# Where the tiles of a two-layer diffusion backbone start in SBUF: small tiles gathered ahead of the weights, large tiles at multiples of 512 bytes

## The chip, the cores and the metric

One NeuronCore of a Trainium2 chip runs the whole program, in one launch. The metric is the device time of that launch in microseconds; the kernel before was timed three times, and the median is given. The profile is of one further execution, which has a time of its own. PE is the matrix engine (PEld its weight loads, which run beside its matmuls), DVE the vector engine, ACT the scalar engine, POOL GpSimd; SP only issues DMAs.

## The reference

Two layers are computed over 256 latent tokens (`x`) and, through the same weights in layer 0, 256 context tokens (`ctx`), each token 1024 wide in fp32. A conditioning vector makes nine modulation rows per layer (`ada_w`, 1024 x 9216). Each sub-layer has the same frame:

```python
def half_step_ffn(x, shift, scale, gate, w_in, w_out, g, b):
    y = swiglu_ffn(modulate(x, shift, scale), w_in, w_out)   # h @ w_in -> silu(a) * u -> @ w_out
    return post_norm_update(x, y, gate, 0.5, g, b)           # layer_norm(alpha * x + 0.5 * gate * y, g, b)
```

A layer is FFN, mixer, FFN. The mixer of layer 0 is a 2-D neighbourhood attention of 16 heads over latent and context keys, that of layer 1 a gated convolution of width 3. The FFN weights are 1024 x 5632 and 2816 x 1024, four times; the two mixers have 1024 x 3072 and 1024 x 1024 each. The output is the latent stream.

## The kernel before

**Products.** Every large product is done in three matmuls: both factors are split into a rounded part (`h`) and a remainder (`l`), and high by high, high by low and low by high are added up in PSUM. In `mmu` (L153, matmuls at L157, L158 and L160) the stationary operand is a 128 x 128 block of the transposed activations (`hTh`, `hTl`, later `gh`, `gl`, `oT`, `yh`, `yl`) and the moving operand is 128 x 512 of weights. In `f0_mm` (L544, matmuls at L549 to L551), the first FFN's first product, it is the other way round: a 128 x 128 block of weights is stationary, and 128 x 512 of activations (`h0h`, `h0l`, 512 tokens at once) moves. Nearly all of PE's time is these six lines.

**Weights.** `wunit` (L163) brings a unit of weights: 256 rows by 512 columns as a tile of 128 partitions x 4096 bytes. A DMA fills the raw tile `wr`, ACT rounds it into the high tile (L179), DVE subtracts for the low tile (L182). The raw tile comes from a ring of 4 buffers, the high and low ones from rings of 5, all in the pool `wp`. Some units take another pair of buffers instead, `whx` and `wlx`, in the pool of the current phase (L167 to L169). In phase 0 (layer 0's first FFN) it is one unit in six, in phase 1 (the attention) none, and in phase 2 (all after it) three in eight. A unit serves 24 of the matmuls of phase 0 in a row of six at a time, and 12 of those of phase 2, six for each of the two latent tiles.

**What else runs.** The modulation rows are streamed in the background: 512 KB of `ada_w` a step, multiplied and added up on DVE (L248). PE's instructions stand in the order that the code writes (L80 has it scheduled by hand); SP, ACT, DVE and POOL are ordered by priorities.

**SBUF.** A pool lies where the pools opened before it end; inside a pool the tags lie in the order of their first tile, each as many bytes per partition as its tiles need (rounded up to 32), times its buffers. The pools in order are `cp` (constants), `wp` (weights), `ap` (38 activation buffers of 2048 bytes, `act`), `sp` (work tiles), and the phase's pool `hp`. So the sizes of the small tiles decide where the large ones start. In the built program, the constants begin at byte 16512 of each partition, and the starts, as remainders of 512, are:

| tiles (bytes per partition) | start, remainder of 512 |
|---|---|
| `ident` (512), the identity for transposes | 128 |
| raw, high and low weights in `wp` (4096 each) | 320 |
| all 38 buffers of `ap` (2048 each): `x`, `hTh`, `hTl`, `gh`, `gl`, `h0h`, `h0l`, `gate` ... | 320 |
| `s2` and `tmp` work tiles in `sp` (2048) | 320 |
| small tiles in `sp`: `mrow`, `stats`, `gcol`, `mv`, `rs` | various |
| phase pool, phases 0 and 2: `whx`, `wlx` (4096), `acc`, `ar`, gates, `xc` | 128 |
| phase pool, phase 1: `bias`, `kr` | 128 |
| phase pool, phase 1, behind the six small `mx` tiles: `pr`, `pT`, `oT` | 320 |

Blocks of 128 columns inside a tile are 512 bytes apart and columns of 512 are 2048, so each operand of a matmul has the remainder of its tile.

Of the kernel before, what the change touches and what calls it, by code (L numbers as in the profile page):

```python
# [9 lines left out]
F32 = mybir.dt.float32  # L10
# [6 lines left out]
P = 128  # L17
D = 1024
FF = 2816
KC = D // P  # L20
# [15 lines left out]
T0_EARLY = 40  # L36
LEAD = 5
TAIL = 3
XAT = 1
A_LAG = 2  # L40
A_PRE = 2
# [24 lines left out]
def backbone_kernel(  # L66
# [6 lines left out]
    nc = tc.nc  # L73
    sync = nc.sync
    cp = ctx.enter_context(tc.tile_pool(name="cp", bufs=1))
    wp = ctx.enter_context(tc.tile_pool(name="wp", bufs=3))
    ap = ctx.enter_context(tc.tile_pool(name="ap", bufs=NACT))
    sp = ctx.enter_context(tc.tile_pool(name="sp", bufs=2))
# [3 lines left out]
    hp = phase.__enter__()  # L82
# [6 lines left out]
    def nm(s):  # L89
        uid[0] += 1  # L90
        return f"{s}_{uid[0]}"
# [4 lines left out]
    def bank(tag, s):  # L96
        return pp.tile([P, 512], F32, tag=tag, bufs=PB[tag], name=nm(s))
# [4 lines left out]
    def tpb(s="tp"):  # L102
        return bank("tp", s)
# [42 lines left out]
    def set_background(gen, rate):  # L146
        background[:] = [gen, rate, 0.0]
# [45 lines left out]
        return wunit([(src[:, :, c0:c0 + 256], 0), (src[:, :, c1:c1 + 256], 256)], UK, s)  # L193


    ident = cp.tile([P, P], F32, tag="ident", name="ident")
    make_identity(nc, ident)
    lnc = cp.tile([P, 2], F32, tag="lnc", name="lnc")
# [4 lines left out]
    warm = cp.tile([1, 1], F32, tag="warm", name="warm")  # L203
    nc.gpsimd.memset(warm, 0.0)
    nc.scalar.activation(warm, warm, AF.Silu)
    crow = cp.tile([16, P], F32, tag="crow", name="crow")
    sync.dma_start(crow[0:8], c[0].rearrange("(a b) -> a b", b=P))
    sync.dma_start(crow[8:16], c_ctx.rearrange("(a b) -> a b", b=P))
    pt = tpb("ctp")
    nc.tensor.transpose(pt[:, 0:16], crow, ident[0:16, 0:16])  # L210
    nc.scalar.activation(cst[:, :, 0:2], pt[:, 0:16].rearrange("p (v k) -> p k v", v=2), AF.Silu)
    ones = cp.tile([P, 32], F32, tag="ones", name="ones")
    nc.vector.memset(ones, 1.0)
    sel = cp.tile([P, 4], F32, tag="sel", name="sel")
    idv = ident.rearrange("p (o m e) -> p o m e", o=2, m=2)
    sv = sel.rearrange("p (m v) -> p m v", m=2)
    nc.vector.tensor_tensor(out=sv, in0=idv[:, 0, :, 0:2], in1=idv[:, 1, :, 0:2], op=ALU.add)
    nc.vector.tensor_tensor(out=sv, in0=sv, in1=idv[:, 0, :, 2:3].to_broadcast([P, 2, 2]), op=ALU.add)
    win_sb = cp.tile([P, 64], F32, tag="wmask", name="wmask")
    rope = cp.tile([P, 2, 4, HD], F32, tag="rope", name="rope")  # L220

    scr = [tc.dram_tile([2, 9 * D], F32, name=f"scr{i}") for i in range(2)]
# [50 lines left out]
    def stream(*groups):  # L273
        for g in groups:
            yield from ada(g)
# [12 lines left out]

    def fold_cols(l, v, m, ln):

        r = sp.tile([32, P], F32, tag="mrow", bufs=2, name=nm("mrow"))
        for i, src in enumerate((scr[l][v, (m + 1) * D:(m + 2) * D], scr[l][v, m * D:(m + 1) * D],
                                 ln_g[ln[0], ln[1]], ln_b[ln[0], ln[1]])):
            sync.dma_start(r[8 * i:8 * i + 8], src.rearrange("(a b) -> a b", b=P))

        def rest():
            ps = tpb("mcT")
            nc.tensor.transpose(ps[:, 0:32], r, ident[0:32, 0:32])
            c = sp.tile([P, 6, KC], F32, tag="gcol", bufs=2, name=nm("gcol"))
            nc.vector.tensor_copy(c[:, 0:4].rearrange("p a b -> p (a b)"), ps[:, 0:32])  # L300
            nc.vector.scalar_tensor_tensor(out=c[:, 4], in0=c[:, 0], scalar=1.0, in1=c[:, 2], op0=ALU.add, op1=ALU.mult)
            nc.vector.scalar_tensor_tensor(out=c[:, 5], in0=c[:, 0], scalar=1.0, in1=c[:, 3], op0=ALU.add, op1=ALU.mult)
            nc.vector.tensor_tensor(out=c[:, 5], in0=c[:, 5], in1=c[:, 1], op=ALU.add)
            return c[:, 4], c[:, 5]

        return Late(6, rest)
# [10 lines left out]
            nc.vector.bn_stats(stats, xt)  # L317

    def stat_tile(n=2):
        return sp.tile([P, 3, 6], F32, tag="stats", bufs=6, name=nm("st"))[:, 0:n]  # L320

    def finish_stats(st):
        mv = sp.tile([P, 2], F32, tag="mv", bufs=6, name=nm("mv"))
        nc.vector.bn_aggr(mv, st)
        rs = sp.tile([P, 1], F32, tag="rs", bufs=6, name=nm("rs"))
        nc.gpsimd.tensor_tensor(out=rs, in0=mv[:, 1:2], in1=lnc[:, 0:1], op=ALU.add)
        nc.gpsimd.tensor_tensor(out=rs, in0=rs, in1=lnc[:, 1:2], op=ALU.pow)
        return mv, rs
# [85 lines left out]
    def order_skew(nu):  # L414

        u = [(n, i) for n in range(2) for i in range(nu)]
        o = []
        for i in range(len(u) + LEAD):
            if i < len(u):
                o.append((0, *u[i]))  # L420
            if i >= LEAD:
                o.append((1, *u[i - LEAD]))
        return o

    def order_last(nu):

        return order_skew(nu)[:-TAIL] + [(1, 1, u, c, c + 256) for c in (0, 256) for u in range(nu - TAIL, nu)]

# [54 lines left out]
    def start_step(k0, n):  # L483
# [5 lines left out]
        for a in range(KC // kt):  # L489
            w = start_tile().rearrange("p (k m c) -> p k m c", k=kt, m=2)  # L490
            for i in range(2):
                sync.dma_start(w[:, :, i], bass.AP(ada_w.tensor, ada_w.offset + a * kt * P * 9 * D + i * D + k0 * P,
                                                   [[9 * D, P], [P * 9 * D, kt], [1, m]]))
            if a == (last if k0 else XAT) and k0 % 2 == 0:
                for t in range(4):
# [91 lines left out]
    stats, gates, hTs = {}, [], {}  # L587
    GB = None
    parts = ((0, 4), (4, 8), (8, NP))
    for fh, (p0, p1) in enumerate(parts):  # L590
# [25 lines left out]
        def evac(t, n, bank, fh=fh):  # L616
            if fh < 2:
                residual(bank, xt[t][n], gates[t // 2][n], 0.5, None if fh else ALPHA)
                return
            if n == 0:  # L620
                stats[t] = stat_tile()
            residual(bank, xt[t][n], gates[t // 2][n], 0.5, None, stats[t][:, n])
            if n == 1:
                mv, rs = finish_stats(stats[t])
                hTs[t] = modulated(xt[t], mv, rs, GB[t // 2], F0_LAG[t])

        if fh == 2:
            drain()
            GB = [fold_cols(0, v, 3, (0, 0)) for v in range(2)]
# [182 lines left out]
    def scores(h, qt):  # L812

        ch = h % 8 // 2
        qh, ql = Q[h // 8].get()[ch // 2]
        qs = slice((ch % 2) * 256 + qt * P, (ch % 2) * 256 + (qt + 1) * P)
        kh, kl = KV[h // 4][0].get()[(h % 4) // 2]
        banks = [bank("at", "S") for _ in range(2)]
        for f in range(3):
            for i in range(2):  # L820
                ps = slice(64 * i, 64 * i + 64)
                nc.tensor.matmul(banks[i], (qh, qh, ql)[f][ps, qs], (kh, kl, kh)[f][ps, :], start=f == 0, stop=f == 2)
        res = []
        for i, S in enumerate(banks):
            Sv = S[:, 0:256].rearrange("p (a b) -> p a b", a=4)
            nc.vector.tensor_tensor(out=Sv, in0=Sv, in1=BIAS.pop((h + i, qt)), op=ALU.add)
            mx = hp.tile([P, 3], F32, tag="mx", bufs=6, name=nm("mx"))
            nc.vector.tensor_reduce(out=mx[:, 0:1], in_=S, axis=AX.X, op=ALU.max, negate=True)
            pr = hp.tile([P, 512], F32, tag="pr", bufs=4, name=nm("pr"))
            nc.scalar.activation(pr, S, AF.Exp, bias=mx[:, 0:1], accum_out=mx[:, 1:2])  # L830
            nc.vector.reciprocal(mx[:, 2:3], mx[:, 1:2])
            nc.scalar.activation(pr, pr, AF.Copy, scale=mx[:, 2:3])
            res.append(pr)
        return res
# [39 lines left out]
    hp = phase.__enter__()  # L874
# [4 lines left out]
    def filler():  # L879
        yield from kv_quarter(1, KV)  # L880
        yield from kv_quarter(2, KV)
        yield from q_half(1, Q)
        yield from kv_quarter(3, KV)
# [12 lines left out]
    fill = filler()  # L896
# [13 lines left out]
    for i in range(len(steps) + LAG + V_LAG):  # L910
        if i == NX_AT:
            new_x(0, 0, s2t)
            for t in range(2):
                for h in range(2):
                    sync.dma_start(xscr[t * P:(t + 1) * P, h * 512:(h + 1) * 512], xt[t][h])
        while i + AHEAD < len(steps) and len(KV) <= steps[i + AHEAD][0] // 4:
            fill_some(1)
        if i < len(steps) and i % 2 == 0:
            with tc.high_priority(offset=S_EARLY):
                prs[i], prs[i + 1] = scores(*steps[i])  # L920
            if i % 2 == 0 and i + 2 < len(steps):
                bias_pair(*steps[i + 2])
        credit += rate[min(i, len(rate) - 1)]
        n = int(credit)
        credit -= n
        if i >= 24 and fin is None:
            run(fill)
            fin = last_filler()
            fill = islice(fin, 9)
        fill_some((n + 1) // 2)  # L930
        if 0 <= i - LAG < len(steps):
            with tc.high_priority(offset=P_EARLY):
                probs_T(*steps[i - LAG], prs.pop(i - LAG))
        fill_some(n // 2)
        j = i - LAG - V_LAG
        if j >= 0 and steps[j][1] == 1:
            with tc.high_priority(offset=V_EARLY):
                values(steps[j][0])
# [5 lines left out]
    hp = phase.__enter__()  # L944
# [8 lines left out]


    set_background(stream([(1, 7, 0)]), 0.4)
    srow = cp.tile([24, P], F32, tag="srow", name="srow")
    sync.dma_start(srow, sc_conv[0].rearrange("j (k p) -> (j k) p", p=P))
    taps = cp.tile([P, 3, KC], F32, tag="taps", name="taps")

# [111 lines left out]
```

## Time and profile before

| | |
|---|---|
| median of 3 runs | 1283.75 us (1282.92 to 1287.06) |
| the profiled execution: time, span | 1283.45 us, 1281.7 us |
| PE busy | 1255.1 us (98%), 5890 matmuls |
| DVE, ACT, POOL busy | 954.6 us (74%), 591.2 us (46%), 42.7 us (3%) |
| DMA | 268.59 MB, mean 210 GB/s |

The span runs from the first to the last instruction; 1.75 us of the execution's time lie around it. Matmuls are pipelined, so one's duration (392 ns or so) overlaps its neighbours', and PE's busy share says only that it never rests. How fast PE goes is read from the distance of the starts of neighbouring matmuls, the pitch, in the timeline, whose first column is the start of a row in microseconds; a row that ends in x2 holds two instructions.

### The profile page before, as it was taken

The page shows a single profiled execution, that of the slowest core. Times are in us where ns is not written, and L with a number is a line of the kernel's source. Part 1 is how long each engine was busy: PE and PEld are TensorE (multiplying, and loading weights), DVE is VectorE, ACT ScalarE, POOL GpSimd, SP SyncE. Part 2 cuts the span into 40 slices and gives each one's busy share as a digit, 9 for nine tenths or more (in the row PEclk, how much of TensorE's full clock was granted, in tenths as well). Part 3 has the DMA queues.
Part 4 walks back from the last instruction along what each step waited for, and adds up shares of the span by engine and source line. Part 5 has one row for each costly group of instructions (what it writes and reads, how often), then busy time and mean ns, then how long its engine had stood idle before and what let it go on. Part 6 is the DMA issues. An engine that isn't in the chain of part 4 may idle for free.

```text
span 1281.7 us, 17190 instructions
## 1 busy us (share of the span) xinstructions
PE 1255.1 (98%) x5890; PEld 1005.4 (78%) x5890; DVE 954.6 (74%) x1683; ACT 591.2 (46%) x1148; POOL 42.7 (3%) x71
## 2 busy tenths in 40 slices
PE   7999999999999999988999999999999999999997
PEld 4787778788778777766787787887788877788886
DVE  3699878495658777788998788867778787865545
ACT  2432132413236456686556435655435744655431
POOL 0000000000001111120000000000000000000000
PEclk9999999999999999999999999999999999999999
DMA  9977569394622744464999887777886754776641
GB/s 291 301 232 238 181 194 307 123 306 133 204 71 83 216 91 91 92 149 133 307 336 313 307 289 271 233 225 228 290 285 221 247 194 131 226 220 188 229 154 51
DMA packets 202713, 268.59 MB, mean 210 GB/s; under 512 B 30027, under 2 KB 149299, under 8 KB 202625
## 3 DMA queue, kind: packets, MB, share of 16 engines
q1 hardware_dynamic: 202624, 267.49, 65.8%
q8 instruction: 46, 0.75, 0.2%
q14 instruction: 43, 0.34, 0.1%
HBM read 265.27 MB, written 2.17 MB: 209 GB/s over the span
## 4 chain that ended last, share of the span: by engine, by line
PE 87%; DVE 5%; DMA 3%; ACT 3%; issue 1%; POOL 0%; SPq 0%; DVEq 0%; ACTq 0%
PE w L157 16%; PE w L158 16%; PE w L160 16%; PE f L549 6%; PE f L550 6%; PE f L551 6%; PE wkv L157 2%; DMA w1r<-in_ffn_w_in_dram 2%; PE wkv L158 2%; PE wkv L160 2%; PE wc L157 2%; PE wc L158 2%; PE wc L160 2%; DMA ar<-in_ada_w_dram 2%; PE gT L408 1%
## 5 line engine op out<-in xcount | busy, mean ns | idle before, releaser
L179 ACT ACTIVATE w1h<-w1r 128x512 fp32r<-128x512 f32 x352 | 202.6, 625 | 181.4 <-PE w L160 68.8
L182 DVE TENSOR_TENSOR w1l<-w1r,w1h 128x512 fp32r<-128x512 f32 x352 | 227.8, 687 | 65.9 <-ACT w1h L179 63.5
L157 PE MATMUL w<-w1h,hTh 128*128 128x512 f32 x528 | 210.8, 399 | 1.4 <-ACT hTh L106 1.4
L248 DVE SCALAR_TENSOR_TENSOR acc<-ar,cst,acc 128x512 f32<-128x512 f32 x266 | 187.5, 749 | 29.4 <-DMA ar<-in_ada_w_dram 29.4
L158 PE MATMUL w<-w1l,hTh 128*128 128x512 f32 x528 | 207.0, 392 | 0.0
L157 PE MATMUL w<-w2h,gh 128*128 128x512 f32 (+1 forms) x446 | 175.4, 394 | 0.0
L158 PE MATMUL w<-w2l,gh 128*128 128x512 f32 (+1 forms) x446 | 173.6, 390 | 0.0
L179 ACT ACTIVATE w2h<-w2r 128x512 fp32r<-128x512 f32 x176 | 101.5, 624 | 140.2 <-PE w L160 129.4
L160 PE MATMUL w<-w1h,hTl 128*128 128x512 f32 x528 | 163.5, 391 | 0.7 <-DVE hTl L107 0.6
L182 DVE TENSOR_TENSOR w2l<-w2r,w2h 128x512 fp32r<-128x512 f32 x176 | 114.2, 688 | 43.9 <-ACT w2h L179 42.6
L549 PE MATMUL f<-h0h,w1h 128*128 128x512 f32 x352 | 139.6, 396 | 0.4 <-ACT w1h L179 0.4
L551 PE MATMUL f<-h0l,w1h 128*128 128x512 f32 x352 | 138.2, 393 | 0.0
L550 PE MATMUL f<-h0h,w1l 128*128 128x512 f32 x352 | 138.2, 393 | 0.0
L160 PE MATMUL w<-w2h,gl 128*128 128x512 f32 (+1 forms) x446 | 136.3, 387 | 0.0
L157 PEld LDWEIGHTS w<-w1h,hTh 128*128 128x128 f32 x528 | 99.2, 188 | 25.4 <-ACT hTh L106 2.7
L160 PEld LDWEIGHTS w<-w1h,hTl 128*128 128x128 f32 x528 | 98.9, 188 | 24.2 <-DVE hTl L107 1.9
L158 PEld LDWEIGHTS w<-w1l,hTh 128*128 128x128 f32 x528 | 99.2, 188 | 20.4 <-DVE w1l L182 0.3
L157 PEld LDWEIGHTS w<-w2h,gh 128*128 128x128 f32 x446 | 83.8, 188 | 21.7 <-issue 1.7
L160 PEld LDWEIGHTS w<-w2h,gl 128*128 128x128 f32 x446 | 83.3, 188 | 18.8
L158 PEld LDWEIGHTS w<-w2l,gh 128*128 128x128 f32 x446 | 83.7, 188 | 18.0 <-DVE w2l L182 0.7
L549 PEld LDWEIGHTS f<-h0h,w1h 128*128 128x128 f32 x352 | 66.4, 189 | 18.3 <-issue 3.8
L551 PEld LDWEIGHTS f<-h0l,w1h 128*128 128x128 f32 x352 | 66.3, 188 | 14.7 <-DVE h0l L527 0.3
(178 smaller groups left out, 1703.1 us busy)
## 6 DMA issues: line engine op xcount, KB each, us to landing
w1r<-in_ffn_w_in_dram SPq DMA_DIRECT2D x352, 256.0 KB
ar<-in_ada_w_dram SPq DMA_DIRECT2D x128, 512.0 KB
w2r<-in_ffn_w_out_dram SPq DMA_DIRECT2D x88, 512.0 KB
ar<-in_ada_w_dram SPq DMA_DIRECT2D x32, 256.0 KB
wkvr<-in_na_w_qkv_dram SPq DMA_DIRECT2D x32, 256.0 KB
wcr<-in_sc_w_in_dram SPq DMA_DIRECT2D x32, 256.0 KB
wqr<-in_na_w_qkv_dram SPq DMA_DIRECT2D x8, 512.0 KB
bias<-in_na_rpb_dram SPq DMA_DIRECT2D x64, 64.0 KB
```

The costliest lines, as they stand in the source:

```text
L157: nc.tensor.matmul(ps, lh, rh, start=first and i == 0, stop=False)
L158: nc.tensor.matmul(ps, lh, rl, start=False, stop=False)
L160: nc.tensor.matmul(ps, ll, rh, start=False, stop=last and i == n - 1)
L179: nc.scalar.activation(hi[:, a:a + m // W_HI], raw[:, a:a + m // W_HI], AF.Copy)
L182: nc.vector.tensor_tensor(out=lo[:, a:b], in0=raw[:, a:b], in1=hi[:, a:b].bitcast(F32), op=ALU.subtract)
L248: nc.vector.scalar_tensor_tensor(out=a, in0=src, scalar=sc, in1=a, op0=ALU.mult, op1=ALU.add)
L408: nc.tensor.transpose(ps[:, j * 256 + i * P:j * 256 + (i + 1) * P], g[:, j * P:(j + 1) * P], ident)
L549: nc.tensor.matmul(ps, lh, hT0[k][0], start=(k == 0), stop=False)
L550: nc.tensor.matmul(ps, ll, hT0[k][0], start=False, stop=False)
L551: nc.tensor.matmul(ps, lh, hT0[k][1], start=False, stop=(k == KC - 1))
```

## The change

A new pool `sm` is opened between `cp` and `wp`. The small tiles `mrow`, `stats`, `gcol`, `mv`, `rs` (from `sp`) and `mx` (from the phase pool) are allocated there, with the buffers that they had. A tile `fill` of 48 floats, which nothing writes or reads, makes up the rest to a multiple of 512. In `cp`, `win_sb` and `ones` are allocated first, so that `ident` starts at a multiple of 512, and the two rows `crow` and `srow`, of the program's start and of layer 1's mixer, share one buffer.

```diff
@@ -36,6 +36,7 @@
+PAD = 48
@@ -73,6 +74,7 @@
     cp = ctx.enter_context(tc.tile_pool(name="cp", bufs=1))
+    sm = ctx.enter_context(tc.tile_pool(name="sm", bufs=1))
     wp = ctx.enter_context(tc.tile_pool(name="wp", bufs=3))
@@ -193,6 +195,10 @@
+    sm.tile([P, PAD], F32, tag="fill", name="fill")
+    win_sb = cp.tile([P, 64], F32, tag="wmask", name="wmask")
+    ones = cp.tile([P, 32], F32, tag="ones", name="ones")
     ident = cp.tile([P, P], F32, tag="ident", name="ident")
@@ -203,20 +209,18 @@
-    crow = cp.tile([16, P], F32, tag="crow", name="crow")
+    crow = cp.tile([24, P], F32, tag="row", name="crow")[0:16]
...
-    ones = cp.tile([P, 32], F32, tag="ones", name="ones")
...
-    win_sb = cp.tile([P, 64], F32, tag="wmask", name="wmask")
@@ -288,7 +292,7 @@
-        r = sp.tile([32, P], F32, tag="mrow", bufs=2, name=nm("mrow"))
+        r = sm.tile([32, P], F32, tag="mrow", bufs=2, name=nm("mrow"))
...
-            c = sp.tile([P, 6, KC], F32, tag="gcol", bufs=2, name=nm("gcol"))
+            c = sm.tile([P, 6, KC], F32, tag="gcol", bufs=2, name=nm("gcol"))
...
-        return sp.tile([P, 3, 6], F32, tag="stats", bufs=6, name=nm("st"))[:, 0:n]
+        return sm.tile([P, 3, 6], F32, tag="stats", bufs=6, name=nm("st"))[:, 0:n]
...
-        mv = sp.tile([P, 2], F32, tag="mv", bufs=6, name=nm("mv"))
+        mv = sm.tile([P, 2], F32, tag="mv", bufs=6, name=nm("mv"))
...
-        rs = sp.tile([P, 1], F32, tag="rs", bufs=6, name=nm("rs"))
+        rs = sm.tile([P, 1], F32, tag="rs", bufs=6, name=nm("rs"))
@@ -824,7 +828,7 @@
-            mx = hp.tile([P, 3], F32, tag="mx", bufs=6, name=nm("mx"))
+            mx = sm.tile([P, 3], F32, tag="mx", bufs=6, name=nm("mx"))
@@ -953,7 +957,7 @@
-    srow = cp.tile([24, P], F32, tag="srow", name="srow")
+    srow = cp.tile([24, P], F32, tag="row", name="srow")
```

No instruction is added, removed or moved. The two built programs have the same 11,152 instructions in the same order on every engine, DMA issues included, with the same shapes, the same offsets inside their tiles, and the same waits and signals. What differs is the address of tiles in SBUF. After the change the weights begin at byte 24064, which is 47 x 512, and every tile of 1024 bytes or more except `cst` and `rope`, which only small work reads, has the remainder 0: `ident`, the weights in `wp` and in `whx` and `wlx`, all of `ap`, `s2`, `tmp`, `acc`, `ar`, the gates, `bias`, `kr`, `pr`, `pT` and `oT`. The rows `mrow` have it too.

## Prediction

> **What bounds the kernel now.** I read the page first: the busy shares and the chain of work that ended last.
>
> ```profile
> PE 1255.1 (98%) x5890; PEld 1005.4 (78%) x5890; DVE 954.6 (74%) x1683; ACT 591.2 (46%) x1148; POOL 42.7 (3%) x71
> PE 87%; DVE 5%; DMA 3%; ACT 3%; issue 1%; POOL 0%; SPq 0%; DVEq 0%; ACTq 0%
> ```
>
> PE is the bound: it hardly rests, and 87% of the chain is PE's own work. A change that only moves addresses can help or hurt in two ways. It can change how long PE needs from one matmul to the next, or how long another engine or a transfer takes. The second counts only on the other 13%. The table of windows says how much room the others have.
>
> ```profile
> core 0: us, PE busy (x) PEld busy (x) DVE busy (x) ACT busy (x) POOL busy (x), PEclk, DMA share, GB/s
> 16.00:32.00 16.00, 16.00 (x120) 11.29 (x123) 7.82 (x19) 4.28 (x9) 0.00 (x0) 1.00 1.05 338
> 600.00:660.00 60.00, 58.54 (x264) 46.75 (x263) 56.26 (x98) 35.28 (x71) 1.07 (x2) 1.00 0.93 310
> 660.00:740.00 80.00, 80.00 (x367) 63.93 (x366) 67.06 (x115) 40.18 (x77) 0.00 (x0) 1.00 0.91 318
> 900.00:1050.00 150.00, 150.00 (x678) 120.67 (x678) 120.36 (x208) 77.09 (x147) 2.14 (x4) 1.00 0.75 250
> ```
>
> In most stretches PE is busy throughout at a granted clock of 1.00, while DVE and the DMA engines have a fifth or a quarter to spare. The tightest place is 600 to 740 us, with DVE at 56.26 of 60 us and the DMA engines at 0.91 to 0.93.
>
> So the question is the pitch, and whether it depends on where operands start. The program before answers in part, since its tiles start at two remainders of 512. Nearly all start at 320; the extra weight pairs of phases 0 and 2 start at 128. First the timeline of PE in the first FFN. All moving operands are at 320 there. The six matmuls from 65.32 have their stationary weights in the extra pair, at 128; those before and after them have both operands at 320.
>
> ```profile
> 63.96 0.39 PE L549 MATMUL f<-h0h,w1h 128*128 128x512 f32 x1
> ...
> 65.32 0.40 PE L549 MATMUL f<-h0h,w1h 128*128 128x512 f32 x1
> ...
> 66.72 0.39 PE L549 MATMUL f<-h0h,w1h 128*128 128x512 f32 x1
> ...
> 68.11 0.39 PE L549 MATMUL f<-h0h,w1h 128*128 128x512 f32 x1
> ...
> 69.47 0.39 PE L549 MATMUL f<-h0h,w1h 128*128 128x512 f32 x1
> ```
>
> Between neighbouring rows here stand six matmuls. Like with like they take 1.36 us (63.96 to 65.32), which is 226.7 ns each. The six with different remainders take 1.40 us, 233 ns each. The next six, like with like again, take 1.39 us, and only the six after them are back at 1.36. So a visit to the extra pair costs 0.04 + 0.03 = 0.07 us per six matmuls, 11.7 ns for each mixed one, half of it paid just after.
>
> The extra pairs also lie in another part of SBUF (above byte 179,000) than the rings (38,000 to 79,000), and that could be the cause. The output product of the attention tells the two apart, in the next rows of the timeline. From 593.53 its stationary tiles `oT` lie above byte 216,000, in the same part as the extra pairs, but at remainder 320, as its weights do.
>
> ```profile
> 592.17 0.39 PE L157 MATMUL wo<-woh,oT 128*128 128x512 f32 x1
> ...
> 593.53 0.39 PE L157 MATMUL wo<-woh,oT 128*128 128x512 f32 x1
> ...
> 597.16 0.61 PE L160 MATMUL wo<-woh,oT 128*128 128x512 f32 x2
> ```
>
> From 592.17 to 593.53 are six matmuls with both operands in the lower part, 1.36 us. From there to 597.16 are sixteen with the distant operand, 3.63 us, 226.9 ns each. No step shows where the region changes. It is the remainder that costs, not the region.
>
> **The change part by part.** *Same start for all operands (the term that counts).* In phase 2 the weights move and the activations are stationary. Two runs of 48 matmuls between transposes show the price. By the addresses of the built program, 30 of the first 48 take their weights from the extra pairs, and 6 of the second.
>
> ```profile
> 701.00 0.48 PE L157 MATMUL w<-w1h,hTh 128*128 128x512 f32 x1
> ...
> 711.70 0.62 PE L160 MATMUL w<-w1h,hTl 128*128 128x512 f32 x2
> ...
> 712.51 0.48 PE L157 MATMUL w<-w1h,hTh 128*128 128x512 f32 x1
> ...
> 723.07 0.62 PE L160 MATMUL w<-w1h,hTl 128*128 128x512 f32 x2
> ```
>
> Over the same 46 distances the first run takes 10.70 us and the second 10.56. That is 0.14 us for 24 more mixed matmuls, 5.8 ns each. Next, how many there are, from the groups by line with shapes kept apart:
>
> ```profile
> L157 PE MATMUL w<-w1h,hTh 128*128 128x512 f32 x528 | 210.8, 399 | 1.4 <-ACT hTh L106 1.4
> L157 PE MATMUL w<-w2h,gh 128*128 128x512 f32 x434 | 172.3, 397 | 0.0
> L549 PE MATMUL f<-h0h,w1h 128*128 128x512 f32 x352 | 139.6, 396 | 0.4 <-ACT w1h L179 0.4
> L157 PE MATMUL wkv<-wkvh,hTh 128*128 128x512 f32 x128 | 52.6, 411 | 0.0
> L157 PE MATMUL wc<-wch,hTh 128*128 128x512 f32 x96 | 38.5, 401 | 0.0
> L157 PE MATMUL wo<-woh,oT 128*128 128x512 f32 x32 | 14.0, 437 | 0.9 <-ACT oT L106 0.9
> L157 PE MATMUL wo<-woh,yh 128*128 128x512 f32 x32 | 12.9, 404 | 0.0
> L157 PE MATMUL wq<-wqh,hTh 128*128 128x512 f32 x32 | 13.2, 412 | 0.0
> ```
>
> Each row stands for a third of its product's matmuls, so there are 3 x (528 + 434 + 352 + 128 + 96 + 32 + 32 + 32) = 4902 of 512 columns. A unit serves 8 matmuls of L549 in phase 0, so 352 / 8 = 44 units; with the 22 of that FFN's second product, 66. One in six is 11 units of 24 matmuls, 264 mixed ones. In phase 2 a unit serves 4 of L157: 132 units of `w1` (528 / 4), 24 of `wc`, 8 of `wo`, and 66 of the second products, 230 in all. Three in eight is 86 units of 12, 1032 mixed ones. Phase 1 has none.
>
> The sum: 264 x 11.7 ns = 3.1 us and 1032 x 5.8 ns = 6.0 us, together 9.1 us of PE. After the change every one of these operands has the remainder 0, so there is no mixed pair left. I take the pitch of 0 with 0 to be that of 320 with 320, since both operands shift by the same amount; this no row shows, and the rivals below price it. Of PE's gain I count the 87% of the chain that is PE's own, as a faster PE waits sooner for the rest: 7.9 us. If all of it counts, 9.1; if half is lost, 4.5.
>
> *Transposes.* `ident` moves from 128 to 0, and what it meets from 320 or 128 to 0.
>
> ```profile
> L844 PE MATMUL PT<-ident,pr 128*128 128x128 f32 x128 | 19.2, 274 | 0.8 <-DVE pT L107 0.5 <-DVE kTl L107 0.2
> L343 PE MATMUL hT<-ident,x 128*128 128x128 f32 x80 | 10.8, 276 | 1.7 <-DVE x L335 1.6
> L781 PE MATMUL kT<-ident,kr 128*128 128x128 f32 x32 | 4.4, 276 | 2.0 <-DVE pT L107 2.0
> L343 PE MATMUL hT<-ident,xc 128*128 128x128 f32 x16 | 2.1, 273 | 0.0
> ```
>
> `pr` and `x` start at 320, `kr` and `xc` at 128 as `ident` does. Mixed they take 274 and 276 ns, alike 276 and 273: no difference in either direction. For some 480 transposes the bounds are 3 ns either way, 1.4 us; I take nothing.
>
> *Vector and scalar work.* The same addition at the two starts:
>
> ```profile
> L313 DVE TENSOR_TENSOR xc<-xc,res 128x512 f32<-128x512 f32 x8 | 5.5, 692 | 0.2
> L313 DVE TENSOR_TENSOR x<-x,res 128x512 f32<-128x512 f32 x8 | 5.5, 691 | 0.1
> ```
>
> `xc` is at 128 with `res` at 320, `x` and `res` both at 320: 692 and 691 ns. DVE does not see the start. I take nothing for it, nor for ACT, and DVE's spare time covers 1 ns on any of its work.
>
> *Transfers.* No row separates transfers by where they land. The windows that DMA fills carry 338 GB/s at a share of 1.05 and 318 at 0.91, 322 and 349 per full share, 4% to either side of their mean. On the 3% of the chain that is DMA (38 us) that is 1.5 us either way; I take nothing. The Trainium skill speaks for a little more here. "DMA: Bandwidth & Descriptors", section "How a descriptor splits into AXI transactions", has a descriptor that does not start at a multiple of 256 bytes pay for the bytes from the boundary below. By it a row of 1024 bytes that starts 64 above one would cost 34 beats and not 32; as an estimate that is 6% of the 38 us, 2.3 us more gain. No run here shows it yet.
>
> *The rest.* The fill tile is never touched. `crow` is read once, at the start, and `srow` is loaded in layer 1's mixer, so sharing a buffer makes nobody wait, and the waits in the program are the same.
>
> So 1283.45 - 7.9 = 1275.55 us for the profiled execution. The median stands 0.3 us above that execution, which gives **1275.9 us**. A measurement of this kernel can tell about 0.3% from no change, 3.9 us.
>
> **The rivals.**
>
> *The start itself is what costs, not the difference (slower).* In the first FFN the weights at 128, a multiple of 128, were slow; 320 is not a multiple of 128, and 0 is. If a stationary operand that starts at a multiple of 128 bytes is slow whatever moves, all 4902 matmuls go at 233 ns. The 4902 - 1296 that are not mixed now would each pay the 6.7 ns that the six at 65.32 pay: 24 us, of which 87% is 21, so 1305. It decides at the six matmuls from 65.32: still 1.40 us after the change, and 1.40 for their neighbours too. For it speaks that no row has both operands at such a start in a large matmul. Against it: transposes with both at 128 are no slower than mixed ones, and in the runs of phase 2 the stationary operand is always at 320 and the mixed run is slower all the same. Chance 0.08.
>
> *The start does not matter, or the gain is eaten (no change).* If the six slow matmuls are slow for another property of the extra pair, or if PE's gain of 9.1 us turns into waits for DVE and DMA as in 600 to 740, the time stays at 1283.5. Against the first stand the rows from 593.53. Against the second, PE is busy for all of 900 to 1050 with DVE at 80%. The Trainium skill has a rule that would bring this about: "TensorE: Matmul & The Clock Gate", section "Step-by-step: what each phase is for", gives PE two independent read ports, so that loading the next weights takes nothing from the running matmul. By that rule the relation of the two starts could not matter; the 1.40 us against 1.36 disagrees. Chance 0.14.
>
> *A start at 0 shortens every matmul (much faster).* If a row of 2048 bytes that starts 64 bytes past a multiple of 128 is read as 17 pieces of 128 and an aligned one as 16, the pitch falls by 1/17, from 226.7 to 213.4 ns. On 4902 matmuls that is 65 us; with the mixed term 74, of which 87% is 65, so 1219. DVE at 56.26 of 60 would not let all of it through. Against it: in phase 2 moving operands at 128 are aligned so already and go slower, not faster. The Trainium skill, "TensorE: Matmul & The Clock Gate", section "Wait — 56ns, not 53.3ns?", states 215.7 ns for 512 columns back to back; an estimate by it is 11 ns on each of the 4902, at 87% 47 us, so 1237. Chance 0.06.
>
> **How the numbers follow.** The forecast has 0.72. Its own range is 1274 (all 9.1 us and a little from transfers) to 1279 (half lost). The range given goes from 1269, for a pitch or transfers somewhat better than at 320, to 1284.3, which takes in no change with the spread of the runs; that leaves out the slow rival and the much faster one, 0.14. Faster by over 0.3%, below 1279.9: 0.69 of the forecast's 0.72 and 0.06, so 0.75. Within 0.3%: 0.14 and the forecast's worst end 0.03, so 0.17. Slower: 0.08.
>
> **What would show it.** In the timeline after: sixes in the first FFN at 1.36 us everywhere, none at 1.40; the runs of 48 matmuls in phase 2 all alike, at 10.53 us or a little less for 46 distances; the attention's pure stretches unchanged at 226.7 ns. DVE's and ACT's means should stay within 1 ns. A pitch at 233 throughout would prove the forecast wrong towards slower, one below 224 towards faster; an unchanged pattern of fast and slow runs would prove the reason wrong.

## The result and the profile after

The changed kernel takes 1276.47 us (median of 6 runs, 1275.29 to 1277.77), beside 1284.72 us of the kernel before in the same comparison (6 runs, 1282.92 to 1287.06). The ratio is 0.9934, with a 95% interval from 0.9921 to 0.9947: 8.25 us, or 0.66%, faster. The forecast was 1275.9.

The profiled execution of the kernel after took 1277.77 us, the slowest of its six runs. First its page: the span, the engines' busy time and the chain.

```profile
span 1276.0 us, 17190 instructions
...
PE 1247.6 (98%) x5890; PEld 1004.9 (79%) x5890; DVE 955.0 (75%) x1683; ACT 591.2 (46%) x1148; POOL 42.1 (3%) x71
...
PE 75%; DVE 10%; DMA 8%; ACT 3%; issue 2%; SPq 1%; POOL 0%; DVEq 0%; ACTq 0%
```

PE's busy time fell from 1255.1 to 1247.6 us, by 7.5. DVE and ACT need what they needed. The span fell by 5.7 us only, since PE rested for 28.4 us in this execution (1276.0 - 1247.6) and for 26.6 in that of before.

Now the sixes of the first FFN, in PE's timeline. Six matmuls stand between neighbouring rows.

```profile
62.71 0.39 PE L553 MATMUL f<-h0h,w1h 128*128 128x512 f32 x1
...
64.07 0.39 PE L553 MATMUL f<-h0h,w1h 128*128 128x512 f32 x1
...
65.43 0.39 PE L553 MATMUL f<-h0h,w1h 128*128 128x512 f32 x1
...
66.79 0.39 PE L553 MATMUL f<-h0h,w1h 128*128 128x512 f32 x1
```

Every step is 1.36 us; the 1.40 and 1.39 of before are gone. Next, two runs of 48 matmuls between transposes in phase 2 (first row and the 47th matmul of each), with rows from the second run that are six matmuls apart.

```profile
698.84 0.47 PE L159 MATMUL w<-w1h,hTh 128*128 128x512 f32 x1
...
709.40 0.62 PE L162 MATMUL w<-w1h,hTl 128*128 128x512 f32 x2
...
710.21 0.48 PE L159 MATMUL w<-w1h,hTh 128*128 128x512 f32 x1
...
711.68 0.40 PE L159 MATMUL w<-w1h,hTh 128*128 128x512 f32 x1
...
713.07 0.39 PE L159 MATMUL w<-w1h,hTh 128*128 128x512 f32 x1
...
714.42 0.39 PE L159 MATMUL w<-w1h,hTh 128*128 128x512 f32 x1
...
720.77 0.62 PE L162 MATMUL w<-w1h,hTl 128*128 128x512 f32 x2
```

Both runs take 10.56 us for 46 distances, where before it was 10.70 and 10.56. Within a run the pace still settles: the six from 711.68 take 1.39 us, the next six 1.35.

The windows of the tightest place and of the long stretch in phase 2:

```profile
core 0: us, PE busy (x) PEld busy (x) DVE busy (x) ACT busy (x) POOL busy (x), PEclk, DMA share, GB/s
...
600.00:660.00 60.00, 58.73 (x267) 47.69 (x267) 56.23 (x98) 33.04 (x66) 1.07 (x2) 1.00 0.96 314
...
900.00:1050.00 150.00, 149.53 (x681) 120.64 (x680) 118.57 (x206) 76.87 (x146) 2.14 (x4) 1.00 0.74 249
```

The clock is granted in full as before. In 150 us PE now issues 681 matmuls and not 678. DMA stands at 0.96 (0.93 before) in the tight window, and PE rests no longer there. In 900 to 1050 us PE rests 0.47 us where it rested none. In these two windows little of the gain is eaten.

To weigh whole programs I use one sum throughout. PE's timeline has 4778 pairs of neighbouring matmuls with 512 columns. Of these, some 4630 lie 218 to 245 ns apart; the rest hold a wait or a break. What the distances of those have above 226.67 ns (1.36 us / 6), added up, is called the **excess** below.

| kernel | phase 0 | phase 1 | phase 2 | excess, us |
|---|---|---|---|---|
| before | 3.42 | 1.19 | 7.35 | 11.96 |
| after | 0.48 | 1.15 | 2.22 | 3.85 |

The difference is 8.1 us; the medians of this comparison show 8.25.

### The profile page after: what moved, and what is told of

Read it like the earlier page. It is cut to its first block, busy times and chain, and to the rows that moved or that the text cites. A ratio compares the mean times of both kernels' runs of the same rounds, so it can differ in the third digit from the quotient of the medians.

```text
span 1276.0 us, 17190 instructions
## 1 busy us (share of the span) xinstructions
PE 1247.6 (98%) x5890; PEld 1004.9 (79%) x5890; DVE 955.0 (75%) x1683; ACT 591.2 (46%) x1148; POOL 42.1 (3%) x71
## 4 chain that ended last, share of the span: by engine, by line
PE 75%; DVE 10%; DMA 8%; ACT 3%; issue 2%; SPq 1%; POOL 0%; DVEq 0%; ACTq 0%
PE w L159 12%; PE w L162 12%; PE w L160 12%; PE f L553 6%; PE f L554 6%; PE f L555 6%; DMA ar<-in_ada_w_dram 5%; DVE w1l L184 3%; DMA w1r<-in_ffn_w_in_dram 2%; PE wkv L159 2%; PE wkv L160 2%; PE wkv L162 2%; PE wc L159 2%; PE wc L162 2%; PE wc L160 2%
```

## The experiments

The theory: PE's pitch depends on whether its two operands start alike, and alignment to 512 bytes has no part in it. The first rival: multiples of 512 are what helps, in PE or in the transfers. A second one came up in the runs: which differences cost, and how much.

**The old kernel with like starts.** The kernel before, with an empty tile ahead of the tiles of phases 0 and 2.

```
+    hp.tile([P, 48], F32, tag="hpad", name="hpad0")
...
+    hp.tile([P, 48], F32, tag="hpad", name="hpad2")
```

> The kernel before, with one empty tile of 192 bytes ahead of the tiles of phases 0 and 2, so that the extra weight pairs start at remainder 320 like all other large tiles. No small tile moves, nothing lies at a multiple of 512. Theory (only a difference between the starts of the two operands costs): all of the change's gain, 1276.5 us or 0.993 to 0.994 of before; all sixes of the first FFN at 1.36 us, the runs of 48 in phase 2 all alike. Rival (multiples of 512 are what helps, in PE or in the transfers): no gain, 1284.5. A split between the two: something between, as 1280.

Measured: 1280.14 us (5 runs, 1277.08 to 1283.86), ratio to before 0.9952 [0.994, 0.9965]. The excess is 3.68 us, and the sixes in its timeline:

```profile
63.55 0.39 PE L550 MATMUL f<-h0h,w1h 128*128 128x512 f32 x1
...
64.91 0.39 PE L550 MATMUL f<-h0h,w1h 128*128 128x512 f32 x1
...
66.27 0.39 PE L550 MATMUL f<-h0h,w1h 128*128 128x512 f32 x1
```

All are 1.36 us. All that PE gains in the kernel after, it gains here with no large tile at a multiple of 512. Yet the median is 3.7 us above the kernel after, whose 1276.5 us were expected, with a wider spread. Its profiled execution, the slowest of the five, shows one place where such time goes: a wait in the attention, where the edit touches nothing (who waited for whom, total us, times, longest).

```profile
PE o L858 <- DVE pT L108: 3.8, 3, 2.8
```

In the kernel after the same wait is 2.3 us shorter:

```profile
PE o L861 <- DVE pT L109: 1.5, 3, 0.6
```

**All large tiles at 320.** The kernel after with a fill tile of 512 bytes.

```
-PAD = 48
+PAD = 128
```

> The kernel after, with a fill tile of 512 bytes in place of 192, so that all large tiles start at remainder 320, the pool of small tiles and the identity as in the kernel after. Theory: as the kernel after, 1276.5 us (ratio to before 0.993 to 0.994), sixes at 1.36 us. Rival (multiples of 512 help): back at 1284.5, or partly, if the transfers gained from them (1278 to 1279 by the 2 us that were estimated for their descriptors).

Measured: 1279.12 us (6 runs, 1275.60 to 1280.29), ratio 0.9948 [0.9935, 0.9962], excess 3.40 us. PE's pitch is that of the kernel after, so the rival falls for PE. For the time it leaves a question, as this median also stands 2.6 us above the kernel after, with overlapping intervals. The runs with raw tiles below take it up.

**The old difference in the new kernel.** An empty tile ahead of the tiles of phases 0 and 2 puts only the extra pairs and their neighbours to 320.

```
+    hp.tile([P, 80], F32, tag="hpad", name="hpad0")
...
+    hp.tile([P, 80], F32, tag="hpad", name="hpad2")
```

> The kernel after, with one empty tile of 320 bytes ahead of the tiles of phases 0 and 2: the extra weight pairs start at 320, all rings and activations stay at 0. Theory: the old difference is back, and with it the old time, 1284 to 1285 us (ratio to before 0.999 to 1.001), six matmuls in the first FFN at 1.40 us for each visit to the extra pair. Rival (most operands at a multiple of 512 is what counts): five sixths of phase 0 and five eighths of phase 2 keep their gain, 1278 to 1280.

Measured: 1284.17 us (12 runs), ratio 0.9998 [0.9984, 1.0012], excess 12.04 us (before: 11.96). The timeline has a visit to the extra pair as before:

```profile
68.86 0.39 PE L554 MATMUL f<-h0h,w1h 128*128 128x512 f32 x1
...
70.22 0.39 PE L554 MATMUL f<-h0h,w1h 128*128 128x512 f32 x1
...
71.60 0.39 PE L554 MATMUL f<-h0h,w1h 128*128 128x512 f32 x1
...
73.00 0.39 PE L554 MATMUL f<-h0h,w1h 128*128 128x512 f32 x1
...
74.37 0.39 PE L554 MATMUL f<-h0h,w1h 128*128 128x512 f32 x1
...
75.73 0.39 PE L554 MATMUL f<-h0h,w1h 128*128 128x512 f32 x1
```

The steps are 1.36, 1.38, 1.40, 1.37 and 1.36 us: 0.07 us for the visit. The pool of small tiles, the aligned identity and alignment of most operands together bring nothing that shows once the difference is back; the interval is 0.14% to either side.

**Nearly everything mixed.** An empty tile ahead of the activations. The extra pairs move with them, so their visits are now the like ones.

```
+    ap.tile([P, 48], F32, tag="apad", bufs=1, name="apad")
```

> The kernel after, with one empty tile of 192 bytes ahead of the activations: weights of the rings stay at 0, activations, temporaries and the extra pairs start at 192. Now the visits to the extra pairs are the like ones and all others mixed: 1320 matmuls in phase 0, 1725 in phase 2, some 560 in phase 1. Theory: at 6 to 7 ns each 20 to 24 us of PE, of which 87% or more counts, so 1294 to 1300 us, slower than before by about 1%. In the first FFN the sixes on the rings take 1.40 us and those on the extra pair less. Rival (alignment to 512 is what counts): the weights keep it and the activations lose it, so at most the time of before, 1284.5.

Measured: 1290.17 us (5 runs), ratio 1.0035 [1.0023, 1.0047]; slower than before, as the theory has it, but by less. The excess is 17.97 us, 14.1 above the kernel after, and the medians, from two comparisons, stand 13.7 apart. Beside the kernel before in its own comparison (1285.26 us) it is 4.9 us slower, with 6.0 us more excess.

```profile
62.26 0.40 PE L554 MATMUL f<-h0h,w1h 128*128 128x512 f32 x1
...
63.66 0.40 PE L554 MATMUL f<-h0h,w1h 128*128 128x512 f32 x1
...
65.06 0.40 PE L554 MATMUL f<-h0h,w1h 128*128 128x512 f32 x1
```

On the rings the first FFN goes at 1.40 us, as expected. What was mis-sized is phase 2: its mixed matmuls on the rings, once in long stretches, run at 229.5 ns (mean of 1636), 2.8 above 226.7 and not 6. So the price of a mixed matmul isn't one number. That led to the runs on single differences.

**Differences of 64 and 128.** Both empty tiles, of 64 bytes (activations) and of 128 (extra pairs).

```
+    ap.tile([P, 16], F32, tag="apad", bufs=1, name="apad")
...
+    hp.tile([P, 32], F32, tag="hpad", name="hpad0")
```

> The kernel after with two empty tiles: the rings' weights at 0, activations at 64, extra weight pairs at 192, so a difference of 64 bytes for the rings and of 128 for the extra pairs. One look at the pitch, to see which differences cost. Theory A (any difference costs alike): nearly all matmuls of the first FFN at 233 ns, six in 1.40 us on rings and extra pairs alike. Theory B (the price goes by the difference within some power of two, 64 or 128): one of the two classes at 226.7 ns and six in 1.36 us, the other at 233. Time by A some 16 us above the kernel after.

Measured: 1294.51 us, one run, 17.8 above the kernel after on the same chip; the excess is 25.92 us, 22.1 above it. Neither theory holds. First the FFN in its timeline, then a run of 48 in phase 2:

```profile
58.01 0.39 PE L555 MATMUL f<-h0h,w1h 128*128 128x512 f32 x1
...
59.38 0.39 PE L555 MATMUL f<-h0h,w1h 128*128 128x512 f32 x1
...
717.57 0.48 PE L160 MATMUL w<-w1h,hTh 128*128 128x512 f32 x1
...
728.38 0.63 PE L163 MATMUL w<-w1h,hTl 128*128 128x512 f32 x2
```

In the FFN, where the activations move, 64 bytes cost little (1.37 us for six). In phase 2, where the weights move, the same 64 bytes the other way (42 of the 48 matmuls of this run; the other six are at 128) make the run 10.81 us where like starts have 10.56. The sign counts.

**Differences of 256 and 64.**

```
+    ap.tile([P, 64], F32, tag="apad", bufs=1, name="apad")
...
+    hp.tile([P, 16], F32, tag="hpad", name="hpad0")
```

> The kernel after with the activations at 256 and the extra weight pairs at 320, rings at 0: differences (start of the moving operand less that of the stationary one) of +256 in the first FFN and -256 in phase 2 on the rings, -64 and +64 on the extra pairs. If the price goes by the signed difference, as the runs so far suggest (+64 cost 2 ns in the first FFN, -64 cost 7 ns in phase 2, +192 7 ns, -192 3 ns): the extra pairs near 233 ns in the first FFN and near 229 in phase 2, and the same price for both phases on the rings, as +256 and -256 are the same within 512. If it goes by the product and not by the difference: first FFN and phase 2 differ on the rings as well.

Measured: 1283.63 us, one run; before, in the same comparison, 1284.52.

```profile
63.51 0.39 PE L555 MATMUL f<-h0h,w1h 128*128 128x512 f32 x1
...
64.87 0.40 PE L555 MATMUL f<-h0h,w1h 128*128 128x512 f32 x1
...
66.27 0.39 PE L555 MATMUL f<-h0h,w1h 128*128 128x512 f32 x1
...
67.66 0.39 PE L555 MATMUL f<-h0h,w1h 128*128 128x512 f32 x1
...
69.02 0.39 PE L555 MATMUL f<-h0h,w1h 128*128 128x512 f32 x1
```

On the rings the operands lie 256 bytes apart, and the six cost 1.36 us: a difference of 256 is free. Only the extra pairs cost, 1.40 and 1.39 us, step for step as in the kernel before. There the difference was +192 in the first FFN, here it is -64; the two are the same within 256. The excess agrees too, 12.15 us against 11.96.

**Differences of 128 and 32.**

```
+    ap.tile([P, 32], F32, tag="apad", bufs=1, name="apad")
...
+    hp.tile([P, 8], F32, tag="hpad", name="hpad0")
```

> The kernel after with the activations at 128 and the extra weight pairs at 160, rings at 0: differences of +128 in the first FFN and -128 in phase 2 on the rings, -32 and +32 on the extra pairs. If the price goes by the signed difference: the rings near 232 ns in both phases (+128 and -128 each gave 232 to 233 on the extra pairs of an earlier run). A difference of 32 costs something if any difference does, and nothing if the starts count only in steps of 64.

Measured: 1296.43 us, one run; the excess is 27.40 us. In the FFN the six take 1.40 us. The run of phase 2, 18 of whose 48 matmuls are at -128 and 30 at +32, takes 10.78:

```profile
57.80 0.39 PE L555 MATMUL f<-h0h,w1h 128*128 128x512 f32 x1
...
59.20 0.39 PE L555 MATMUL f<-h0h,w1h 128*128 128x512 f32 x1
...
707.82 0.48 PE L160 MATMUL w<-w1h,hTh 128*128 128x512 f32 x1
...
718.60 0.63 PE L163 MATMUL w<-w1h,hTl 128*128 128x512 f32 x2
```

Together the runs give the pitch by the signed difference, start of the moving operand less start of the stationary one, within 256 (so +128 and -128 are one row, and +192 is -64). The means leave out the first 14 matmuls after a break; behind each stand the number of distances and where they are from.

| difference within 256 | pitch, ns |
|---|---|
| 0 | 226.7 (3261, after) |
| +64 | 228.9 (753, differences of 64 and 128, FFN), 229.5 (1636, nearly everything mixed, phase 2) |
| +128 | 232.5 (753, FFN) and 232.6 (1635, phase 2), differences of 128 and 32 |
| -64 | 233.4 (753, nearly everything mixed, FFN), 233.3 (1635, differences of 64 and 128, phase 2) |
| -32 and +32 | 232.5 (118) and 233.0 (749), extra pairs, differences of 128 and 32 |

**The kernel after once more, and all at 32.** The first is unchanged; the second has a fill tile of 208 bytes.

> The kernel after, unchanged, on the chip of the next runs. The kernels with every large tile at remainder 320 gave 1280.1 and 1279.1 us on another chip, this one 1276.5 on its own, with intervals that overlap. Theory (only sameness counts; the rest is the spread of the waits for transfers): within 0.2% of the kernel with all large tiles at 32, and somewhere from 1276 to 1280. Rival (multiples of 512 help the transfers besides): 1276.5 again, 2 to 3 us below the kernel at 32.

```
-PAD = 48
+PAD = 52
```

> The kernel after with a fill tile of 208 bytes in place of 192: the allocator then puts all large tiles at remainder 32, a multiple of no 64. Theory: PE's pitch as in the kernel after (sixes 1.36 us, excess of the pitch over 226.7 ns summed over the large matmuls 3.4 to 3.9 us), time within 0.2% of the kernel after. Rival (the transfers gain from multiples of 512): same pitch, but 1279, more waiting of PE for weights.

Measured on one chip: for the kernel after 1276.76 us (5 runs, 1274.65 to 1278.61; 0.9938 [0.9925, 0.9951]) and for all at 32 1278.33 us (5 runs, 1276.17 to 1279.89; 0.9951 [0.9939, 0.9963]). The excess is 3.81 and 3.29 us, so at 32 PE loses nothing, and for PE a start at a multiple of no 64 is as good as one at 0. The times differ by 0.12%, within both intervals.

**The identity at 128.** The identity is taken ahead of the mask and the ones again; the large tiles stay at 0.

```
+    ident = cp.tile([P, P], F32, tag="ident", name="ident")
     win_sb = cp.tile([P, 64], F32, tag="wmask", name="wmask")
     ones = cp.tile([P, 32], F32, tag="ones", name="ones")
-    ident = cp.tile([P, P], F32, tag="ident", name="ident")
```

> The kernel after with the identity allocated ahead of the mask and the ones: it starts at 128 again, all large tiles stay at 0. So the 480 or so transposes are mixed and nothing else changes. Theory: the transposes do not see it (0 to 1.4 us), 1276 to 1278 us. Rival (the transposes share the price of the large matmuls, or carry it into the dozen matmuls behind them): 480 transposes at 6 ns and the matmuls behind, 3 us or more, 1279.5 or above.

Measured: 1277.10 us (6 runs, 1274.58 to 1281.22), ratio 0.9945 [0.993, 0.996], beside 1276.76 of the kernel after on the same chip. Its groups of transposes:

```profile
L848 PE MATMUL PT<-ident,pr 128*128 128x128 f32 x128 | 19.2, 274 | 0.9 <-DVE pT L109 0.5 <-DVE kTl L109 0.2
...
L785 PE MATMUL kT<-ident,kr 128*128 128x128 f32 x32 | 4.9, 294 | 2.0 <-DVE pT L109 2.0
```

Mixed now, the 128 transposes of `pr` take 274 ns each. The 32 of `kr` take 294 where the kernel after has 276, 0.6 us in all. Their time doesn't go by the difference as that of the large matmuls does: 256 bytes from the identity (differences of 256 and 64) `kr` takes 289 ns, 320 bytes from it (all but the raw tiles at 320) 276. The excess is 4.04 us (after: 3.81). So the identity's place is worth under 1 us.

**Only the landing place of the weights.** In the first kernel the fill tile moves behind the raw tiles, so that they alone start at 320; in the second 320 bytes are put there, so that they alone start at 0. The edit shown is the first one.

```
-    sm.tile([P, PAD], F32, tag="fill", name="fill")
+    rawpad = []
...
+        if not rawpad:
+            rawpad.append(wp.tile([P, 48], F32, tag="rawpad", bufs=1, name="rawpad"))
```

> The kernel after, where only the buffers into which the large weights are loaded (the raw tiles) start at remainder 320; everything that PE reads stays at 0 (the fill tile of 192 bytes moves behind the raw tiles). Three kernels with all large tiles at 320 or 32 gave 1278.3 to 1280.1 us, the kernel after 1276.5 and 1276.8, with the same pitch of PE. If the last 2 us are those of transfers that land at a multiple of 512: 1278 to 1280 here. If they are spread, or hang on something else than the landing place: 1276 to 1277.5. PE's pitch as in the kernel after by both.

> The mirror: only the raw tiles start at remainder 0, everything else that is large at 320. If the landing place of the weights gives the last 2 us: 1276 to 1277.5, as the kernel after. If it doesn't: 1278 to 1280, as the kernel with all at 320. Pitch as in the kernel after by both.

Measured: 1276.23 us (5 runs, 1275.13 to 1276.68; 0.9932 [0.9918, 0.9945]) with the raw tiles at 320, and 1276.77 us (6 runs, 1275.19 to 1279.31; 0.9943 [0.9927, 0.9958]) with all but them at 320. The excess is 3.65 and 3.22 us. Weights that land at 320 cost nothing that shows. The second kernel is as fast as the kernel after though every large tile that PE reads starts at 320. So neither the landing place of the weights nor the start of PE's operands by itself gives the 1.6 to 3.7 us by which three other kernels with like starts stood above the kernel after; the smaller landing tiles, and the waits that change from execution to execution, weren't told apart.

## Why the prediction was right

*PE is the bound and the pitch is what the change moves.* Right: the excess fell by 8.1 us and the medians by 8.25. The forecast was a gain of 7.9.

*The difference of remainders costs, not the region.* Right, and shown from both sides: the extra pairs stay where they are in the old kernel and lose their price when their start is shifted by 192 bytes (1.36 us in every six), and in the new kernel the price returns with the difference (12.04 us of excess, ratio 0.9998). Only the modulus was taken too wide: 256 bytes apart is as good as alike.

*The sum.* For phase 0 I had 3.1 us; measured 3.42 - 0.48 = 2.94. For phase 2 I had 6.0; measured 7.35 - 2.22 = 5.13, or 5.0 ns for each of the 1032. The price of 5.8 ns came from 24 more mixed matmuls between two runs. The second of these, with 6 mixed ones, took 10.56 us, exactly what a run with none takes now, so the 0.14 us belonged to 30 of them and not 24: 4.7 ns. And a mixed matmul doesn't pay all of it itself. In phase 2 of the kernel before, 3.50 us of the excess lie in the 985 distances behind mixed matmuls and 3.85 in the 1629 behind like ones, 2.4 ns each; in the kernel after the mean over all of them is 0.85 ns. So about half of the price falls on like matmuls, which fits the 2.8 ns of mixed matmuls in long stretches: changing from one kind to the other costs too. Phase 1 had none mixed and kept its excess, 1.19 and 1.15.

*The 87% of the chain.* The runs neither confirm nor refute this discount. In this comparison the medians show all of the 8.1 us, but the interval, 6.8 to 10.1 us, takes in 87% of it as well. Over the eight comparisons of kernels with like starts (the kernel after twice, like starts in the old kernel, all at 320, all at 32, the identity at 128, and the two of the raw tiles) the medians fell by 5.1 to 8.3 us and the excess by 7.9 to 8.7: on the mean 7.1 of 8.3 us, or 0.85. The two slowest kernels, of one run each, point the same way. The one with differences of 64 and 128 has 22.1 us more excess and 17.8 us more time than the kernel after on the same chip. The one with differences of 128 and 32 has 23.7 us more excess and 20.2 us more time than the kernel with the raw tiles at 320. PE rests 25.3 us in both, and 28.4 and 27.9 in two profiled executions of the kernel after, but 29.2 with nearly everything mixed. PE's share of the chain is 75% in the profiled execution of the kernel after and 85% in another of the same kernel, so one such share doesn't measure what comes through:

```profile
PE 85%; DVE 6%; DMA 4%; ACT 3%; issue 1%; SPq 0%; POOL 0%; DVEq 0%; ACTq 0%
```

That the forecast came within 0.6 us is partly luck. The 9.1 us of PE were 1.0 too many, the discount took 1.2 off, and kernels with the same pitch gave medians from 1276.2 to 1280.1 us.

*Transposes, vector work.* Right for this change. The groups of the kernel after:

```profile
L848 PE MATMUL PT<-ident,pr 128*128 128x128 f32 x128 | 19.7, 278 | 0.9 <-DVE pT L109 0.5 <-DVE qTl L109 0.2 <-DVE kTl L109 0.2
...
L347 PE MATMUL hT<-ident,x 128*128 128x128 f32 x80 | 10.9, 277 | 2.0 <-DVE x L339 1.8
L317 DVE TENSOR_TENSOR xc<-xc,res 128x512 f32<-128x512 f32 x8 | 5.5, 690 | 0.2
L317 DVE TENSOR_TENSOR x<-x,res 128x512 f32<-128x512 f32 x8 | 5.5, 689 | 0.1
...
L785 PE MATMUL kT<-ident,kr 128*128 128x128 f32 x32 | 4.4, 276 | 2.0 <-DVE pT L109 2.0
```

`hT` went from 276 to 277 ns, `kT` stayed at 276, `PT` from 274 to 278, the two additions from 692 and 691 to 690 and 689. The 4 ns of `PT` and the 2 ns of the additions are just outside the bounds of 3 and 1 ns, but a second profiled execution of this kernel has 274, 690 and 692, so they are the spread between executions.

*Transfers.* Right to take nothing: weights that land at 320, 64 above a multiple of 256, gave 1276.23 us, no slower than the kernel after. The Trainium skill's rule on descriptors that don't start at a multiple of 256 bytes ("DMA: Bandwidth & Descriptors", section "How a descriptor splits into AXI transactions") speaks of bytes that are fetched. Here only the place where the data lands moved, and there the 2.3 us that the prediction estimated from it don't show.

*The rivals.* The start itself as the cost fell: sixes at 0 and 0 take 1.36 us, not 1.40. A start at 0 that shortens every matmul fell too: 226.7 ns at 0, 32 and 320 alike. No change fell with the result. The Trainium skill's independent read ports ("TensorE: Matmul & The Clock Gate", section "Step-by-step: what each phase is for") would make the relation of the two starts irrelevant; the table of differences, 226.7 to 233.4 ns, disagrees.

*What was to be seen.* Sixes at 1.36 us everywhere: seen. Runs of 48 at 10.53 us or less: alike, but at 10.56. The attention's output product unchanged at 226.7 ns: six matmuls in 1.36 us between the rows of the kernel after,

```profile
591.23 0.39 PE L159 MATMUL wo<-woh,oT 128*128 128x512 f32 x1
...
592.59 0.39 PE L159 MATMUL wo<-woh,oT 128*128 128x512 f32 x1
```

## What to carry to other kernels

Where matmuls follow each other closely with new weights each time, look at the starts of the moving and the stationary tiles within 256 bytes: alike is the fastest, here at 0, 32 and 320 the same, and one odd buffer in a ring is seen as a step in the distance of starts. The cheap repair is an empty tile of the right size ahead of the odd one, which gave the same pitch as moving all small tiles. Read what PE gains from the distances of starts; how much of it reaches the time, here 0.85 on the mean, is told by timing several kernels of the same pitch, and not by PE's share of one chain.

## What the runs showed of the hardware that was not expected

The price of a difference has a sign: the moving operand 64 bytes further on than the stationary one costs 2.2 to 2.8 ns a matmul, 64 bytes behind it 6.6 to 6.7, and 256 bytes nothing. Even 32 bytes cost about 6 ns. For +32 that holds in longer stretches too. At -32 there were only sixes between mixed ones, and like sixes in such a place take 231.2 ns already (118 distances, nearly everything mixed), so the price of -32 by itself isn't told apart. Why a difference costs, and why its sign counts, no run shows.

PE doesn't return to its pace at once. In phase 2 of the kernel before, the first ten like matmuls behind a visit take 231.4 ns on the mean (487 distances, again without the first 14 after a break), and those from the eleventh on 226.7 (569). In the kernel after, with no mixed pair, the six from 711.68 take 1.39 us and only the next 1.35; a run of 48 takes 10.56 us where 46 distances of 226.7 ns are 10.43. All the excess left, 3.85 us, is of this kind: from the 15th matmul after a break on the mean is 226.7 ns. No experiment tried to remove it, and what sets it is open.
